# A third staging buffer, and one buffer for the transposed maxima and the value rows

## The chip, the cores and the metric

The kernel runs on one core of a Trainium2 chip. The metric is the device time of one execution in microseconds (us). Three timed executions of the kernel before gave 720.60, 721.52 and 723.17 us, so the median is 721.52 us. Times of single instructions and waits come from one further execution that was profiled.

## The reference, cut to what matters

One decoder block on 1024 tokens and 16 meta tokens, with a model width of 1024. Everything is float32.

```python
h = rmsnorm(concat(meta, x), norm_g)                 # 1040 x 1024
proj = h @ w_in                                      # 1040 x 5128
u, z, q, k, v, z_attn, f, g_pool, g_attn = split(proj)
y_pool = causal_multiscale_pool(u, pool_w, pool_scale) * silu(z)
logit[t, s] = q_t.k_s / 8 + sum_{s<j<=t} log_sigmoid(f_j + b)    # 8 heads of 64, causal
y_attn = softmax(logit) @ v * silu(z_attn)
merged = sigmoid(g_pool) * (y_pool @ w_up_pool) + sigmoid(g_attn) * (y_attn @ w_up_attn)
out = rmsnorm(h_residual + merged @ w_out, final_norm_g)          # the 1024 token rows
```

## The kernel before, in words

A float32 product is computed as three reduced-precision products of a high and a low part of each operand, so every operand is split into `hi` and `lo`. A projection of a 128-column chunk of `w_in` (`g_proj`, L170) is 24 matmuls into one PSUM bank. PE's program order is written out by the kernel itself. The other engines' order comes from a scheduler, and each engine works through its own order without overtaking.

**Attention phase** (about 80 to 425 us). The 16 units are (head pair, head of the pair, half of the 1024 queries). For a unit, `qk` (L710, L711) makes the scores of one key block, ACT and DVE bring them into `S`, and DVE keeps a running maximum in a PSUM tile `pt` (L724). Then `maxes` reduces it over the keys:

- DVE transposes the maxima into the SBUF tile `mt` (L729), reduces them (L734), and with small copies by ACT (`mx` L736, `my` L739) and DVE (`mz` L740) makes the column maxima, which DVE transposes back into a PSUM tile (L742).
- `soft` subtracts that (L751), takes the exponential on ACT (L752) and splits the result into `ph` (L756) and `pl` (L757). `av` (L775) multiplies by the values into the PSUM tile `po`.
- `finish` copies `po` into the SBUF tile `t` on ACT (L786; for the last head pair L783 and L784), and SP stores `t` to DRAM in one or two DMAs of 128 KB (L788, `sp_y<-t`). Those are the value rows.

`maxes` of the next unit stands ahead of `finish` of the present one. So in the order of the program each `mt` is followed by a `t`, and the `t` of a unit is stored to DRAM during the whole following unit. `mt` and `t` have one 2 KB buffer each (per partition) in the pool `ap`.

**The filler.** Between the attention matmuls PE works off a list of projections (class `Fill`): for a later head pair `q` (L268, L272), `k` (L286 on ACT, L290 on DVE) and `v`, and, when none of these is due, the pieces of `u` (`f_u`, L357, L359) and of the gates (`f_raw`, L347, L348). A `u` or gate piece is evicted by ACT into a staging tile `st` and stored from there by SP. There are two staging buffers, in the pool `stg`. The filler's PSUM banks are the two of the pool `pj`, so a bank is used again by the second projection after it, once the evictions (for `k` those of L286 and L290) are through.

**After the attention** the pools `ap` and `at` are closed and the pool `bp` takes their place in SBUF. The gate products (L1049) follow. Their first 48 matmuls use weights that were split during the attention phase. The next ones use weights that ACT splits into `gw` (L1004), with the low part from GpSimd (L1011) or DVE (L1008). DVE also transposes and sums the softmax denominators, which SP brings back from DRAM (`zp<-accd`, L955, L960, L961).

DMAs that add in DRAM are issued by GpSimd (L616, L643), each after the transposition `mt` of a unit; ACT issues copies DRAM to DRAM (L612).

The lines that the change touches:

```python
    spill, stores, evacs = {}, [], []                                     # L338
            st = stg.tile([128, 512], F32, name="st")                     # L346, in f_raw
            st = stg.tile([128, 512], F32, name="st")[:, :c1 - c0]        # L356, in f_u
            mt = ap_.tile([KB, 512], F32, name="mt")                      # L728, in maxes
            t = ap_.tile([128, 512], F32, name="t")                       # in finish, as it was
```

Of the kernel before, what the change touches and what calls it, by code (L numbers as in the profile page):

```python
# [8 lines left out]
F32 = mybir.dt.float32  # L9
# [13 lines left out]
KB = 128  # L23
# [30 lines left out]
def tile_hybrid_block(ctx, tc, x, meta, norm_g, w_in, b_forget, pool_w, pool_scale,  # L54
# [21 lines left out]
    stg = ctx.enter_context(tc.tile_pool(name="stg", bufs=2))  # L76
# [3 lines left out]
    ap_ = A.enter_context(tc.tile_pool(name="ap", bufs=1))  # L80
# [81 lines left out]
    def w_chunk(col, **kw):  # L162
        return split_w([w_in2[:, :, col:col + 128]], **kw)
# [20 lines left out]
    def g_proj(w, t0, t1):  # L184
        wh, wl = w
        ps = fill_bank()[:, :t1 - t0]
        yield from g_mm3(ps, [(wh[:, k, :], wl[:, k, :], hh[k][:, t0:t1], hl[k][:, t0:t1]) for k in range(KO)])
        return ps
# [69 lines left out]
    def keys_of(t0, t1):  # L258
        r = [(0, min(t1, SEQ) - t0, t0 + NM)]
        if t1 > SEQ:  # L260
            r.append((SEQ - t0, t1 - t0, 0))
        return [(slice(a, b), slice(d, d + b - a)) for a, b, d in r]
# [72 lines left out]
            if c0:  # L335
                yield from v_blocks(p, *{384: (1, 2), 768: (3, 4, 5)}[c0])

    spill, stores, evacs = {}, [], []  # L338

    def f_raw(key, col):  # L340
        w = w_chunk(col)
        dt = dr.tile([128, SEQ], F32, name=f"sp_{key[0]}{key[1]}")
        spill[key] = dt
        for c0, c1 in HALVES:
            ps = yield from g_proj(w, c0, c1)
            st = stg.tile([128, 512], F32, name="st")  # L346
            evacs.append(nc.scalar.activation(st, ps, AF.Copy))  # L347
            stores.append(nc.sync.dma_start(dt[:, c0:c1], st))  # L348

    def f_u(g):  # L350
        w = w_chunk(COL_U + g * 128)
        dt = dr.tile([128, L], F32, name=f"sp_u{g}")
        spill["u", g] = dt
        for c0, c1 in PIECES:
            ps = yield from g_proj(w, c0, c1)
            st = stg.tile([128, 512], F32, name="st")[:, :c1 - c0]  # L356
            nc.scalar.activation(st, ps, AF.Copy)  # L357
            for c, d in keys_of(c0, c1):
                last = nc.sync.dma_start(dt[:, d], st[:, c])  # L359
            stores.append(last)  # L360
# [314 lines left out]
    class Unit:  # L675
# [49 lines left out]

        def maxes(self, extra=0.0, hook=None):
            F.pull(LM1 + extra)
            mt = ap_.tile([KB, 512], F32, name="mt")  # L728
            tr = nc.vector.transpose(mt, self.m)  # L729
            if hook is not None:  # L730
                hook(tr)
            r, r2 = self.m[:, :16], self.m[:, 16:32]
            x, y, mx = [sm.tile([128, 16], F32, name=n) for n in ("mx", "my", "mz")]
            nc.vector.tensor_reduce(r, mt.rearrange("p (j b) -> p j b", b=32), axis=AX.X, op=ALU.max)  # L734
            for a, b in ((0, 64), (64, 0)):
                nc.scalar.activation(x[a:a + 64], r[b:b + 64], AF.Copy)  # L736
            nc.vector.tensor_tensor(r2, r, x, op=ALU.max)
            for a, b in ((0, 32), (32, 0), (64, 96), (96, 64)):
                nc.scalar.activation(y[a:a + 32], r2[b:b + 32], AF.Copy)  # L739
            nc.vector.tensor_tensor(mx, r2, y, op=ALU.max)  # L740
            self.pm = psT.tile([128, 512], F32, name="pt")
            nc.vector.transpose(self.pm, mx[:, :, None].to_broadcast([128, 16, 32]))  # L742
            F.pull(LM2)
# [62 lines left out]
    for g in (3, 2, 1, 0):  # L806
        F.add_free(f_u(g))
    for key in raws:
        F.add_free(f_raw(key, cols[key[0]] + 128 * key[1]))
# [679 lines left out]
```

## Time and profile before

| what | value |
|---|---|
| median of three timed executions | 721.52 us (720.60 to 723.17) |
| the profiled execution's own time | 722.44 us |
| its span, first to last instruction | 720.4 us |
| PE busy / weight loads busy | 707.4 us (98%) / 610.7 us (85%) |
| DVE / ACT / GpSimd busy | 512.0 / 425.9 / 353.9 us |
| chain that ended last, share of PE | 94% |

The span leaves 2.0 us of the execution's own time outside, before the first and after the last instruction. Rows of the timeline give start, duration, engine, line, operation, output and input tile, and in brackets how long the engine had been idle and what released it. Rows of the waits give who waited for whom, the total, how often, and the longest.

### The profile page before, as it was taken

How to read it: one execution, taken by the hardware profiler on the slowest of the kernel's cores; microseconds unless marked ns; L12 is line 12 of the kernel's file. 1: busy time of each engine (PE TensorE's matmuls, PEld its weight loads, DVE VectorE, ACT ScalarE, POOL GpSimd, SP SyncE). 2: the span in 40 equal slices, each digit the busy share in tenths (PEclk: the TensorE clock that was granted, in tenths of full speed). 3: DMA queues.
4: the chain of work that ended last, by engine and by line, in shares of the span. 5: the costliest groups of instructions: out<-in, count | busy, mean ns of one | idle time of the engine just before them, and what ended most of it. 6: DMA issues, size and time to landing. Idle time of an engine off the chain costs nothing.

```text
span 720.4 us, 10921 instructions
## 1 busy us (share of the span) xinstructions
PE 707.4 (98%) x3613; PEld 610.7 (85%) x3613; DVE 512.0 (71%) x909; ACT 425.9 (59%) x936; POOL 353.9 (49%) x481
## 2 busy tenths in 40 slices
PE   8999999799999999999999999999999999999996
PEld 6997999798889988898888888888888888888885
DVE  5743488477688767787587866899847545888775
ACT  7753577567787867777587614455646332535445
POOL 5412336477377675747388643458951010007152
PEclk9999999999999999999999999999999999999999
DMA  9211225986968889497858768799518366861006
GB/s 308 65 30 30 60 62 199 271 244 193 260 177 230 239 229 281 118 261 214 224 154 206 223 202 318 239 304 308 129 35 273 113 224 233 272 224 60 0 1 233
DMA packets 97482, 134.09 MB, mean 186 GB/s; under 512 B 11809, under 2 KB 63009, under 8 KB 95154
## 3 DMA queue, kind: packets, MB, share of 16 engines
q1 hardware_dynamic: 83296, 94.07, 40.8%
q0 software_dynamic: 2512, 18.35, 13.3%
q10 hardware_dynamic: 11618, 20.98, 8.2%
q8 instruction: 28, 0.46, 0.2%
q14 instruction: 28, 0.23, 0.1%
HBM read 103.29 MB, written 62.59 MB: 230 GB/s over the span
## 4 chain that ended last, share of the span: by engine, by line
PE 94%; ACT 2%; DMA 2%; DVE 1%; issue 1%; POOL 0%; POOLq 0%; ACTq 0%
PE pj L170 55%; PE pj L1049 12%; PE pj L1369 8%; PE po L775 5%; PE pt L1049 4%; PE pt L1369 2%; PE ps L711 2%; DMA sp_u<-st 2%; PE ps L710 2%; PE pj L521 1%; PE pt L232 1%; PE pj L711 1%; PE pj L710 1%; ACT qa L268 1%; PE pn L232 0%
## 5 line engine op out<-in xcount | busy, mean ns | idle before, releaser
L170 PE MATMUL pj<-hh,whi 128*128 128x512 f32 (+3 forms) x576 | 128.3, 350 | 0.0
L170 PE MATMUL pj<-hh,wlo 128*128 128x512 f32 (+3 forms) x576 | 127.1, 346 | 0.0
L170 PE MATMUL pj<-hl,whi 128*128 128x512 f32 (+3 forms) x576 | 126.8, 345 | 0.0
L170 PEld LDWEIGHTS pj<-hh,whi 128*128 128x128 f32 x576 | 98.4, 190 | 10.2 <-ACT hh L234 0.4
L158 POOL TENSOR_TENSOR wlo<-raw,whi 128x256 fp32r<-128x256 f32 x100 | 73.5, 774 | 65.1 <-PE pj L170 24.5
L170 PEld LDWEIGHTS pj<-hh,wlo 128*128 128x128 f32 x576 | 96.8, 188 | 10.0
L765 POOL TENSOR_TENSOR acc<-acc,S 128x256 f32<-128x256 f32 (+2 forms) x128 | 90.3, 723 | 30.5 <-ACT S L752 20.8
L170 PEld LDWEIGHTS pj<-hl,whi 128*128 128x128 f32 x576 | 96.6, 189 | 9.8
L757 DVE TENSOR_TENSOR pl<-S,ph 128x512 fp32r<-128x512 f32 (+4 forms) x112 | 80.5, 736 | 19.4 <-ACT ph L756 18.9
L1011 POOL TENSOR_TENSOR gw<-graw,gw 128x256 fp32r<-128x256 f32 x52 | 53.6, 1056 | 44.2 <-ACT gw L1004 41.8
L1049 PE MATMUL pj<-gh,gw 128*128 128x512 f32 x276 | 64.3, 389 | 0.0
L724 DVE TENSOR_TENSOR pt<-pt,S 128x400 f32<-128x400 f32 (+2 forms) x96 | 46.4, 483 | 22.1 <-ACT S L715 19.6
L1049 PEld LDWEIGHTS pj<-gh,gw 128*128 128x128 f32 x276 | 51.8, 188 | 10.9
L752 ACT ACTIVATE S<-S 128x512 f32<-128x512 f32 (+4 forms) x112 | 50.6, 479 | 8.6 <-DVE S L751 8.4
L756 ACT ACTIVATE ph<-S 128x512 fp32r<-128x512 f32 (+4 forms) x112 | 52.4, 482 | 2.3 <-PE po L775 1.4
L751 DVE TENSOR_TENSOR S<-S,pt 128x512 f32<-128x512 f32 (+4 forms) x112 | 49.7, 498 | 0.6
L1262 DVE TENSOR_TENSOR rl<-pj,rl 128x512 f32<-128x512 f32 x32 | 22.0, 689 | 28.7 <-PE pj L170 28.1
L1004 ACT ACTIVATE gw<-graw 128x512 fp32r<-128x512 f32 x38 | 23.5, 626 | 27.9 <-DMA graw<-gs 12.0
L715 ACT ACTIVATE S<-ps,negc 128x16 f32<-128x16 f32 (+4 forms) x65 | 33.0, 513 | 10.9 <-PE ps L711 10.3
L765 POOL TENSOR_TENSOR acc<-S 128x256 f32<-128x256 f32 (+1 forms) x32 | 28.6, 926 | 21.1 <-ACT S L752 17.5
L136 POOL TENSOR_TENSOR X<-G 128x256 f32<-128x256 f32 x8 | 5.8, 740 | 63.9 <-DVE G L1264 63.9
L775 PE MATMUL po<-ph,V 128*128 128x512 f32 (+4 forms) x112 | 36.6, 327 | 0.3 <-ACT ph L756 0.2
(250 smaller groups left out, 1434.2 us busy)
## 6 DMA issues: line engine op xcount, KB each, us to landing
raw<-in_w_in_dram SPq DMA_DIRECT2D x27, 512.0 KB, 5.9
gs<-in_w_in_dram ACTq DMA_DIRECT2D x15, 512.0 KB, 7.6
gs<-gs POOLq DMA_DIRECT2D x4, 1536.0 KB, 12.7
graw<-gs SPq DMA_DIRECT2D x12, 512.0 KB, 6.1
td<-in_w_out_dram ACTq DMA_DIRECT2D x10, 512.0 KB, 11.4
graw<-in_w_in_dram SPq DMA_DIRECT2D x9, 512.0 KB, 6.9
xt<-in_x_dram SPq DMA_DIRECT2D x8, 512.0 KB, 6.3
accd<-acc SPq DMA_DIRECT2D x16, 256.0 KB, 4.2
```

What stands on the lines that cost most here:

```text
L158: ins = nc.gpsimd.tensor_tensor(lo[:, k:k + 2], raw[:, k:k + 2], r32(hi[:, k:k + 2]), op=ALU.subtract)
L170: nc.tensor.matmul(ps, a, b, start=(i == 0), stop=(i == len(seq) - 1))
L724: nc.vector.tensor_tensor(m[:kb, c0:], m[:kb, c0:], s[:kb, c0:], op=ALU.max)
L751: nc.vector.tensor_tensor(s[:kb, c0:], s[:kb, c0:], self.pm[:kb, c0:], op=ALU.subtract)
L752: exps.append(nc.scalar.activation(s[:kb, c0:], s[:kb, c0:], AF.Exp))
L756: nc.scalar.activation(ph[:kb, c0:], s[:kb, c0:], AF.Copy)
L757: dves.append(nc.vector.tensor_tensor(pl[:kb, c0:], s[:kb, c0:], r32(ph[:kb, c0:]), op=ALU.subtract))
L765: accs.append(nc.gpsimd.tensor_tensor(acc[:kb, c:c1], (S0 if b == 1 else acc)[:kb, c:c1], s[:kb, c:c1], op=ALU.add))
L775: nc.tensor.matmul(self.po[:, c0:], v, self.P[b][i][:kb, c0:], start=(b == 0 and i == 0), stop=(b == self.nb - 1 and i == 1))
L1011: nc.gpsimd.tensor_tensor(op[:, 1, k:k + 2], raw[:, k:k + 2], r32(op[:, 0, k:k + 2]), op=ALU.subtract)
L1049: nc.tensor.matmul(ps, stat(n, i, p, k), op_h[n][q][k // 2][:, k % 2], start=fresh and m == 0, stop=m == 11, skip_group_check=True)
L1369: nc.tensor.matmul(ps, pick(A_, k, p)[:, i * 128:(i + 1) * 128], pick(B_, k, q)[:, c0:c1], start=start and n == 0, stop=n == 11, skip_grou ...
```

## The change

A counter hands out the staging tiles of `f_u` and `f_raw` in turn: two of three from the pool `stg` as before, every third one from a new 2 KB buffer in the pool `ap`. To make room, the tile `mt` of `maxes` takes the tag of the tile `t` of `finish`, so that both now live in one buffer.

```diff
-    spill, stores, evacs = {}, [], []
+    spill, stores, evacs, staged = {}, [], [], [0]
+
+    def stage_in():
+        staged[0] += 1
+        if staged[0] % 3:
+            return stg.tile([128, 512], F32, name="st")
+        return ap_.tile([128, 512], F32, name="st", bufs=1)
...
-            st = stg.tile([128, 512], F32, name="st")
+            st = stage_in()
...
-            st = stg.tile([128, 512], F32, name="st")[:, :c1 - c0]
+            st = stage_in()[:, :c1 - c0]
...
-            mt = ap_.tile([KB, 512], F32, name="mt")
+            mt = ap_.tile([KB, 512], F32, name="mt", tag="t")
```

Lines behind the change have numbers higher by 6 in the changed kernel. The instructions are the same, and on PE, DVE, ACT and GpSimd they stand in the same order. What differs is what they wait for, and one place on SP. Three places show it. In brackets stand the semaphores that a row waits for; those named DMAHW count landed DMAs of SP and ACT.

The first is DVE's order at the twelfth unit's maxima, where a `k` projection's evictions (`ka`) follow the transposition `mt`. Before:

```order
L724 TENSOR_TENSOR pt_3795<-pt_3795,S_3926 128x16 [waits DVE_49]
L729 STREAM_TRANSPOSE mt_4002<-pt_3795 128x512 [waits DVE_49]
L734 TENSOR_REDUCE pt_3795<-mt_4002 128x16 [waits DVE_49]
L290 TENSOR_TENSOR ka_3778<-pj_3854,ka_3778 64x384 [waits PE_49,Activation_49]
L290 TENSOR_TENSOR ka_3779<-pj_3854,ka_3779 64x384
L737 TENSOR_TENSOR pt_3795<-pt_3795,mx_4005 128x16 [waits DVE_49,Activation_49]
```

The same place in the changed kernel:

```order
L730 TENSOR_TENSOR pt_3795<-pt_3795,S_3926 128x16 [waits DVE_49]
L735 STREAM_TRANSPOSE mt_4002<-pt_3795 128x512 [waits DMAHW3_49,DMAHW2_49,DVE_49]
L740 TENSOR_REDUCE pt_3795<-mt_4002 128x16 [waits DVE_49]
L290 TENSOR_TENSOR ka_3778<-pj_3854,ka_3778 64x384 [waits PE_49,Activation_49]
L290 TENSOR_TENSOR ka_3779<-pj_3854,ka_3779 64x384
L743 TENSOR_TENSOR pt_3795<-pt_3795,mx_4005 128x16 [waits DVE_49,Activation_49]
```

The transposition now waits for two landed DMAs, which are the two stores of the `t` before it (L788), because it writes into the buffer that they read. From the third to the sixteenth unit every `mt` has this wait.

The second is ACT's order at the end of the attention phase: the last three gate pieces and the first two weight splits behind them. Before:

```order
L347 ACTIVATE st_5174<-pj_5111 128x512 [waits DMAHW4_49,PE_49]
L347 ACTIVATE st_5213<-pj_5188 128x512 [waits DMAHW7_49,PE_49,Activation_49]
L347 ACTIVATE st_5241<-pj_5216 128x512 [waits DMAHW4_49,PE_49,Activation_49]
L1004 ACTIVATE gw_5320<-graw_5273 128x512 [waits DMAHW5_49,DMAHW6_49,DMAHW1_49,Pool_49]
L1004 ACTIVATE gw_5341<-graw_5273 128x512 [waits DMAHW3_49,DVE_49]
```

The same place in the changed kernel:

```order
L353 ACTIVATE st_5174<-pj_5111 128x512 [waits DMAHW2_49,PE_49]
L353 ACTIVATE st_5213<-pj_5188 128x512 [waits DMAHW4_49,PE_49]
L353 ACTIVATE st_5241<-pj_5216 128x512 [waits DMAHW7_49,PE_49,Activation_49]
L1010 ACTIVATE gw_5320<-graw_5273 128x512 [waits DMAHW3_49,DMAHW1_49,DMAHW5_49,DVE_49,DMAHW6_49,Activation_49,Pool_49]
L1010 ACTIVATE gw_5341<-graw_5273 128x512
```

The last two gate pieces wait for an earlier store than before (the third store back instead of the second). The first `gw` now also waits for the store of the last gate piece, `st_5241` (DMAHW6 here), because the new staging buffer lies under it.

The third is SP's order at the same time. Before:

```order
L348 DMA sp_ga2_5017<-st_5174 128x512
L955 DMA zp_5264<-accd_771 128x1024
L955 DMA zp_5266<-accd_771 128x1024
L348 DMA sp_ga3_5187<-st_5213 128x512
L348 DMA sp_ga3_5187<-st_5241 128x512
L992 DMA graw_5345<-in_w_in_dram 128x4x256
```

The same place in the changed kernel:

```order
L354 DMA sp_ga2_5017<-st_5174 128x512
L354 DMA sp_ga3_5187<-st_5213 128x512
L354 DMA sp_ga3_5187<-st_5241 128x512
L961 DMA zp_5264<-accd_771 128x1024
L961 DMA zp_5266<-accd_771 128x1024
L998 DMA graw_5345<-in_w_in_dram 128x4x256
```

The first two loads of `zp` moved behind the last two gate stores.

## The prediction

> **What bounds the kernel now.** I read the page first, then the waits, then the timelines of the stretches where the change acts. The chain of waits is PE's almost alone, and PE's own list of waits shows how little it stands still (who waited for whom, us in total, times, longest):
>
> ```profile
> PE 94%; ACT 2%; DMA 2%; DVE 1%; issue 1%; POOL 0%; POOLq 0%; ACTq 0%
> PE pj L710 <- ACT S L715: 4.1, 1, 4.1
> PE po L775 <- ACT ph L756: 0.2, 1, 0.2
> ```
>
> So an edit pays only if it removes one of PE's few waits, and it costs as soon as it delays something that PE needs by more than that thing's lead. Staging is waited for here (waits of ACT, then from the rows of the staging line who waited for it):
>
> ```profile
> ACT st L347 <- DMA sp_ga<-st: 11.2, 2, 5.7
>   PEld pj L1049: 0.2, 1
> ```
>
> ACT stood 11.2 us, but in two places only, and PE's weight loads lost 0.2 us by it. ACT and PE at that place:
>
> ```profile
> 425.63 0.60 ACT L347 ACTIVATE st<-pj 128x512 f32<-128x512 f32 x1 [5.54 <-DMA sp_ga<-st]
> 431.92 0.60 ACT L347 ACTIVATE st<-pj 128x512 f32<-128x512 f32 x1 [5.70 <-DMA sp_ga<-st]
> 428.12 1.98 PE L170 MATMUL pj<-hh,wlo 128*128 128x512 f32 x8
> 441.05 1.09 PE L1049 MATMUL pj<-hh,gw 128*128 128x512 f32 x4
> ```
>
> The last projection ends at 430.1 (428.12 + 1.98); the first product on a fresh `gw` starts at 441.05, and in between PE works on weights that were split earlier. ACT splits `gw` right behind its row at 431.92, so `gw` has a lead of over 7 us.
>
> **What the third buffer removes.** The gate piece at 425.63 would wait for PE alone, the last one for PE at 430.1 instead of a landing at 431.9. Nothing that PE needs is late today except that 0.2 us. Gain: 0.2 us, at most.
>
> **What the shared buffer adds.** `mt` must wait until the stores of the previous `t` have landed, and behind `mt` in DVE's queue stands everything else of DVE. The lead is read by setting each pair of stores against the next `mt`. For all pairs together, then for the pairs before 313.8, 273.0 and 233.4, the rows of the store's line give first and last issue, and time to landing (min/median/max):
>
> ```profile
> DMA to landing us min/median/max: 2.4/9.4/17.4
> ...
> L788 SPq DMA_DIRECT2D sp_y<-t x2: 451/564/676, 299.7 to 300.2; - x2
> DMA to landing us min/median/max: 16.3/16.8/17.4
> ...
> L788 SPq DMA_DIRECT2D sp_y<-t x2: 452/918/1384, 258.7 to 259.2; - x2
> DMA to landing us min/median/max: 14.7/14.7/14.7
> ...
> L788 SPq DMA_DIRECT2D sp_y<-t x2: 544/566/587, 219.2 to 219.8; - x2
> DMA to landing us min/median/max: 13.7/13.8/13.8
> ```
>
> DVE at these places, and, at the last of them, ACT's links of the chain and PE's users:
>
> ```profile
> 233.37 0.72 DVE L729 STREAM_TRANSPOSE mt<-pt 128x512 f32<-128x512 f32 x1
> 273.03 0.72 DVE L729 STREAM_TRANSPOSE mt<-pt 128x512 f32<-128x512 f32 x1
> 313.78 0.72 DVE L729 STREAM_TRANSPOSE mt<-pt 128x512 f32<-128x512 f32 x1
> 315.26 1.13 DVE L290 TENSOR_TENSOR ka<-pj,ka 64x384 fp32r<-64x384 f32 x2
> 316.63 0.73 ACT L739 ACTIVATE my<-pt 32x16 f32<-32x16 f32 x4 [1.00 <-DVE pt L737]
> 319.06 0.91 ACT L286 ACTIVATE ka<-pj 64x256 fp32r<-64x256 f32 x4
> 320.00 1.03 DVE L290 TENSOR_TENSOR ka<-pj,ka 64x256 fp32r<-64x256 f32 x4 [0.35 <-ACT ka L286]
> 317.63 1.57 PE L170 MATMUL pj<-hh,whi 128*128 128x384 f32 x8
> 321.81 1.55 PE L170 MATMUL pj<-hh,whi 128*128 128x384 f32 x8
> 321.06 1.14 ACT L756 ACTIVATE ph<-S 128x512 fp32r<-128x512 f32 x2
> 325.06 0.39 PE L775 MATMUL po<-ph,V 128*128 128x512 f32 x1
> ```
>
> *At 313.8.* The later store lands at 300.2 + 17.4 = 317.6, so `mt` starts 3.8 us late. Queued behind it are the two `ka` evictions, which end at 316.4 (315.26 + 1.13) today and at 320.2 then. They free the PSUM bank that PE's next projection wants at 317.63: PE stands 2.6 us. The `ka` at 320.00 follows on `mt` through a chain without slack: DVE's maxima, ACT's `my` at 316.63, which waits for them, ACT's next rows up to its part of `ka` at 319.06, and DVE's wait for that. So it ends at 321.0 + 3.8 = 324.8, and it frees the bank for 321.81: PE's total delay becomes 324.8 − 321.8 = 3.0 us. The first attention product has its `ph` by 322.2 and takes it at 325.06; that lead of 2.9 covers the 0.8 us that DVE and ACT are then later than PE.
>
> *At 273.0.* The later store lands at 259.2 + 14.7 = 273.9: `mt` is 0.9 us late. The way to PE, in rows of ACT and PE:
>
> ```profile
> 277.58 0.63 ACT L752 ACTIVATE S<-S 128x512 f32<-128x512 f32 x1 [0.45 <-DVE S L751]
> 279.63 1.20 ACT L268 ACTIVATE qa<-pj 64x512 fp32r<-64x512 f32 x2 [0.23 <-PE pj L170]
> 290.21 0.63 ACT L756 ACTIVATE ph<-S 128x512 fp32r<-128x512 f32 x1
> 290.90 0.49 PE L775 MATMUL po<-ph,V 128*128 128x512 f32 x1
> ```
>
> ACT's exponential at 277.58 waits for DVE and takes over the 0.9; the idle 0.23 at 279.63 swallows some. From there ACT and DVE follow each other almost without a gap up to `ph`, which ends at 290.84 just before PE takes it at 290.90 (the 0.2 us in PE's list). So about 0.6 us reach PE.
>
> *At 233.4.* Landing at 219.8 + 13.8 = 233.6, 0.2 us late, less than the 0.8 us of lead at the worst place above: nothing. The other stores landed before their `mt`.
>
> The value of 3.8 is the one that this execution shows; it isn't a constant. From below, if the stores at 299.7 took the 14.7 us of the next slowest pair, `mt` would be 1.1 us late and PE 0.3. From above, I allow each landing 1 us more, about a fourteenth of it: the two terms become 4.0 and 1.6 us, 5.6 together.
>
> **What else moves.** The first two `zp` loads go out behind the last gate store, at about 431, and that store must land before the first `gw`. Rows of DVE, of PE, and of the DMA issues between 404 and 480 (KB each, median us to landing):
>
> ```profile
> 433.01 1.25 DVE L960 STREAM_TRANSPOSE zp<-zp 128x1024 f32<-128x1024 f32 x1 [7.77 <-DMA zp<-accd]
> 452.35 0.69 DVE L1060 TENSOR_TENSOR za<-pj,za 128x512 f32<-128x512 f32 x1
> 456.50 1.98 PE L1049 MATMUL pj<-hh,gw 128*128 128x512 f32 x8
> zp<-accd SPq DMA_DIRECT2D x8, 512.0 KB, 5.9
> sp_ga<-st SPq DMA_DIRECT2D x7, 256.0 KB, 4.9
> ```
>
> `zp` lands at about 431 + 5.9 = 437 and DVE's first transposition starts 4 us later than at 433.01. The eviction that PE needs first behind it is that at 452.35, for the bank that it takes within the row at 456.50: 453.0 + 4 is just early enough, and the waits for later `zp` loads in between shrink the 4. The gate store, issued at about 430.9, lands at about 436, so `gw` is ready by 437.5, against 441.05. Both cost nothing, with 3 us of cover for `gw`: were the landing 9.5 us or more, PE would pay what exceeds that.
>
> **The sum**, made on the profiled execution (722.44, 0.9 above the median): −0.2 + 0.6 + 3.0 = +3.4, so 725.8 there, and 721.5 + 3.4 = 724.9 by the median. PE has no later wait that could give it back. About 0.3%, 2.2 us, is what a measurement of this kernel can tell from no change.
>
> **Rivals.**
>
> *The stores land in time.* In the timed executions the two stores before the twelfth `mt` land by 314.5 (in 14.3 us), where the lead of 0.8 us covers the rest. This place decides: below about 16.5 us to landing the loss is under 2.2 us, below 14.3 it is nothing. Time: 721.3 to 723.7, at the same 721.5 if all is covered. For it: the median of all pairs is 9.4 us, and the 17.4 is the largest of all. Against it: 14.7 and 13.8 occur as well, and the order of all DMAs up to there is unchanged. The Trainium skill ("SBUF — State Buffer", The DMA setup-cost knee) puts a transfer at about 2 us plus its bytes over 436 GB/s; by that estimate a 128 KB store lands within 2.3 us, no `mt` ever waits, and the sum is −0.2. The trace's 2.4 to 17.4 us disagree except at their lowest.
>
> *PE's pause drops its clock.* The one long pause of PE is followed by a slower clock (busy times of PE, weight loads, DVE, ACT, GpSimd, then the granted clock, DMA share and GB/s):
>
> ```profile
> 135.00:140.00 5.00, 1.42 (x8) 0.97 (x6) 0.00 (x0) 0.20 (x1) 0.00 (x0) 1.00 0.98 325
> 140.00:145.00 5.00, 4.46 (x15) 4.16 (x16) 2.10 (x3) 4.28 (x9) 1.34 (x3) 0.66 1.07 321
> ```
>
> The wait of 4.1 us cost 5 x (1 − 0.66) = 1.7 us more. A pause of 2.6 us is shorter, and nothing here shows whether it is enough; with it the sum is +5.1, 726.6. The Trainium skill ("TensorE: Matmul & The Clock Gate", Part 1) gives an idle window of about 3.4 us on a free-running grid as the condition; by that rule the 2.6 us would pass unpunished, and a landing 1 us later might not. The 4.1 us agree with it.
>
> *The freed ACT pays.* If PE's pace at 425 to 440 hung on ACT after all, up to 5.5 us could come back, 716 to 719. Against it stand the 0.2 us and PE's unbroken rows there.
>
> **How the numbers follow.** The forecast, a loss of 2.2 to 5.6 us with the clock kept: 0.56, time 724.9. Landing in time: 0.33. Clock dropped or a late gate store: 0.08, 726 to 728.5. The freed ACT: 0.03. The range goes from 721.3 (all covered, 0.2 gained) to 728.5 (the upper bound of both terms, 5.6, and a part of the clock's 1.7). Faster 0.03, same 0.33, slower 0.64. The likeliest case alone spans 723.7 to 727.1.
>
> **What would show it.** In the profile after: a wait of DVE at `mt` for `sp_y<-t` near 313.8 of 3 to 4 us and near 273 of about 1; in PE's waits a new row for DVE's `ka` (L290) of about 2.6 us; PE's later rows all later by about 3.4 us; ACT's waits for `sp_ga<-st` gone or below 2 us, with a wait at `gw` for the last gate store in their place. I am wrong if `mt` shows no wait, or if PE's rows from 430 on are not later than before; if PE waits between 430 and 470, the third part failed.

## The result, and the profile after

The change makes the kernel slower, by more than was forecast: 728.79 us (727.92 to 729.83, four executions) against 721.98 us, a ratio of 1.0088 with a 95% interval of 1.0074 to 1.0101. On another chip it was 730.93 against 723.62 us, 1.0101 (1.0079 to 1.0123). The ratios are estimated from the single executions and are not the quotient of the two medians (here 1.0094); "us slower" below goes by the ratio. Two executions, one each of two experiments, took over 1000 us at a mean granted clock of 0.56 and 0.61, and the ratios leave them out. The forecast was 724.9, with a range up to 728.5.

The profiled execution after took 728.66 us, with a span of 726.7 against 720.4. PE's own list of waits (who waited for whom, us in total, times, longest):

```profile
PE pj L716 <- ACT S L721: 3.3, 1, 3.3
PE po L781 <- ACT ph L762: 2.3, 2, 2.1
PE pj L1055 <- DVE gx L1066: 1.4, 1, 1.4
PE pn L425 <- DVE car L563: 1.3, 1, 1.3
PE pj L170 <- DVE ka L290: 1.2, 2, 1.0
```

The first and the fourth row were there before (4.1 and 1.3). New are a long wait for `ph` (0.2 before), one for `ka`, and one for `gx`, which no step of the prediction had. The timeline of DVE shows where the first two come from, and that of PE where they arrive:

```profile
274.68 0.72 DVE L735 STREAM_TRANSPOSE mt<-pt 128x512 f32<-128x512 f32 x1 [2.37 <-DMA sp_y<-t]
...
318.91 0.72 DVE L735 STREAM_TRANSPOSE mt<-pt 128x512 f32<-128x512 f32 x1 [2.29 <-DMA sp_y<-t]
320.38 1.12 DVE L290 TENSOR_TENSOR ka<-pj,ka 64x384 fp32r<-64x384 f32 x2
```

```profile
292.19 0.50 PE L781 MATMUL po<-ph,V 128*128 128x512 f32 x1 [2.11 <-ACT ph L762]
...
321.65 1.65 PE L170 MATMUL pj<-hh,whi 128*128 128x384 f32 x8 [0.99 <-DVE ka L290]
```

Both transpositions wait for the value stores, at the two units that were named. At the tenth PE pauses 2.1 us where 0.6 was expected, at the twelfth 1.0 where 2.6 was. What followed the first pause is seen in stretches of 2 us (busy times of PE, weight loads, DVE, ACT, GpSimd, then granted clock, DMA share, GB/s):

```profile
290.00:292.00 2.00, 0.08 (x1) 0.00 (x0) 1.60 (x3) 1.98 (x5) 0.51 (x1) 1.00 0.08 27
292.00:294.00 2.00, 1.81 (x8) 1.57 (x9) 2.00 (x6) 2.00 (x8) 1.92 (x3) 0.85 0.00 0
294.00:296.00 2.00, 2.00 (x8) 1.80 (x8) 2.00 (x4) 1.50 (x5) 1.89 (x4) 0.50 0.00 0
296.00:298.00 2.00, 2.00 (x8) 1.67 (x8) 1.93 (x7) 0.00 (x0) 1.87 (x4) 0.80 0.15 56
```

The clock fell to a half for 3.4 us: 2 x (0.15 + 0.50 + 0.20) = 1.7 us lost on top of the pause.

The third new wait lies where the prediction had stopped looking. SP's timeline at the end of the attention phase, first of before, then of after:

```profile
425.81 1.32 SPq L955 DMA_DIRECT2D zp<-accd  x2
...
469.31 0.36 SPq L966 DMA_DIRECT2D sums<-ge  x1
...
476.80 1.94 SPq L970 DMA_DIRECT2D fin<-sums  x4
```

```profile
435.74 0.93 SPq L961 DMA_DIRECT2D zp<-accd  x2
...
475.51 0.48 SPq L972 DMA_DIRECT2D sums<-ge  x1
...
483.42 1.93 SPq L976 DMA_DIRECT2D fin<-sums  x4
```

And DVE, of before and of after, with PE's row of after behind them:

```profile
481.53 0.61 DVE L974 TENSOR_REDUCE fin<-fin 128x64 f32<-128x256 f32 x1 [0.94 <-DMA fin<-sums]
...
483.50 1.28 DVE L1060 TENSOR_TENSOR gx<-pj,gx 128x512 f32<-128x512 f32 x2
```

```profile
440.56 1.25 DVE L966 STREAM_TRANSPOSE zp<-zp 128x1024 f32<-128x1024 f32 x1 [10.75 <-DMA zp<-accd]
...
487.99 0.62 DVE L980 TENSOR_REDUCE fin<-fin 128x64 f32<-128x256 f32 x1 [2.10 <-DMA fin<-sums]
...
489.96 1.28 DVE L1066 TENSOR_TENSOR gx<-pj,gx 128x512 f32<-128x512 f32 x2
```

```profile
490.79 8.44 PE L1055 MATMUL pj<-gh,gw 128*128 128x512 f32 x36 [1.44 <-DVE gx L1066]
```

The first two `zp` loads leave SP 9.9 us later than before, of which 4.6 is the delay that PE has there already. The first transposition of `zp` starts at 440.6 instead of 433.0. The later loads win back part of it, but the sums still go out 6.2 us late and come back 6.5 us late at `fin` (487.99 against 481.53), 1.6 and 1.9 more than PE's own 4.6. In DVE's queue stands `gx` behind `fin`, and PE needs its bank: 1.4 us.

ACT is freed at 425 to 437 as forecast. The last gate piece waits for PE alone, and `gw` waits for that piece's store:

```profile
434.74 0.60 ACT L353 ACTIVATE st<-pj 128x512 f32<-128x512 f32 x1 [4.89 <-PE pj L170]
437.92 1.16 ACT L1010 ACTIVATE gw<-graw 128x512 fp32r<-128x512 f32 x2 [2.58 <-DMA sp_ga<-st]
```

No wait of PE answers to either. In sum: 1.9 + 1.7 at the tenth unit (the 0.2 that PE waited there before taken off), 1.2 at the twelfth, 1.4 at `gx`, less 0.8 at 136 to 140, where a store of `u` happened to land earlier. That makes 5.4 of the 6.3 us. With PE's instructions of the two profiles set against each other one by one, the rest lies mostly at the same places: the twelfth unit adds 1.7 us in all (its second `ka` makes the row at 321.81 of before start at 326.30) and `gx` 1.7.

### The profile page after: what moved, and what is told of

It is laid out like the page before. It is cut to its first block, busy times and chain, and to the rows that moved or that the text cites. A ratio compares the mean times of both kernels' runs of the same rounds, so it can differ in the third digit from the quotient of the medians.

```text
span 726.7 us, 10931 instructions
## 1 busy us (share of the span) xinstructions
PE 710.0 (98%) x3613; PEld 613.1 (84%) x3613; DVE 511.3 (70%) x909; ACT 425.3 (59%) x936; POOL 353.5 (49%) x481
## 4 chain that ended last, share of the span: by engine, by line
PE 87%; DMA 5%; DVE 2%; ACT 2%; issue 1%; SPq 1%; POOL 0%; POOLq 0%; ACTq 0%; DVEq 0%
PE pj L170 52%; PE pj L1055 9%; PE pj L1375 8%; PE po L781 5%; PE pt L1055 3%; DMA sp_y<-t 2%; PE pt L1375 2%; PE ps L717 2%; DMA sp_u<-st 1%; PE ps L716 1%; DMA sums<-ge 1%; PE pj L527 1%; PE pt L232 1%; PE pj L717 1%; PE pj L716 1%
## 6 DMA issues: line engine op xcount, KB each, us to landing
td<-in_w_out_dram ACTq DMA_DIRECT2D x10, 512.0 KB, 11.2
```

## The experiments

Each was timed beside the kernel before on its chip (723.0 to 723.6 us there).

**The change once more.**

> The changed kernel once more, beside the others on one chip. Expected: 5 to 7 us slower than before, as when it was first measured; in its profile the pauses of PE near 290 and 321 again add up to 3 to 5 us, split otherwise than 2.1 and 1.2, and the wait for gx near 490 is between 0 and 3.4 us.

Measured: 1.0101 (1.0079 to 1.0123), 7.3 us slower, a little above what was expected. Its PE list has 2.4 (2.2 the longest) for `ph`, 2.4 for `ka` and 2.5 for `gx`, and of these three pauses only the one for `ka` was followed by a slower clock. The places are the same in both profiles; how much each costs is not.

**The two halves of the change.** One kernel shares the buffer only, the other adds the third buffer only.

```
shared only:   mt = ap_.tile([KB, 512], F32, name="mt", tag="t")     # st as before
third only:    mt = ap_.tile([KB, 512], F32, name="mt", tag="pl", bufs=NPH + 1)
               # st handed out in turn as in the change
```

> Only the shared buffer of mt and t; two staging buffers as before. Theory A (the shared buffer costs most of it): the tenth and the twelfth mt wait for the value stores by 0.9 to 2.5 us and 2.3 to 3.8 us, PE loses about 3.6 us at the first place (1.9 of pause, 1.7 of slower clock, if its pause is as long as in the changed kernel) or 0.6 (if it is as short as forecast) and 1.8 to 3.0 at the second: 3.4 to 5.4 us slower than before, 725.4 to 727.4. Rival B (the third buffer and the new order on SP make things late): at most 1.5 us slower, under 723.5.

Measured: 728.25 us, 1.0070 (1.0058 to 1.0083), 5.1 us slower, with these rows of PE:

```profile
PE pj L710 <- ACT S L715: 4.5, 1, 4.5
PE pj L170 <- DVE ka L290: 3.2, 1, 3.2
PE po L775 <- ACT ph L756: 1.6, 2, 1.5
```

This time the pause at the twelfth unit is the long one, 3.2 us, close to the forecast's 3.0, and the clock fell behind it, not behind the 1.5 us at the tenth.

> Only the third staging buffer: mt takes a place in the ring of pl, whose readers are matmuls, so that mt waits for no store. Theory A: no wait of DVE at mt for a store; what is left is the pair of zp loads behind the gate stores, which comes out at the softmax sums as a wait of PE of 1.4 us near 485: 0.7 to 1.7 us slower than before, 722.7 to 723.7. Rival B: 4 us slower or more, 726 and above.

Measured: 725.16 us, 1.0026 (1.0009 to 1.0043), 1.9 us slower, spread from 721.9 to 730.4 over 12 executions. The profiled one is the slowest of them. Rows of DVE and PE:

```profile
438.55 1.25 DVE L966 STREAM_TRANSPOSE zp<-zp 128x1024 f32<-128x1024 f32 x1 [11.44 <-DMA zp<-accd]
...
487.33 0.58 DVE L980 TENSOR_REDUCE fin<-fin 128x64 f32<-128x256 f32 x1 [3.68 <-DMA fin<-sums]
```

```profile
490.10 10.07 PE L1055 MATMUL pj<-gh,gw 128*128 128x512 f32 x32 [3.44 <-DVE gx L1066]
```

No `mt` waits for a store. Of the 8.2 us that this profile is longer than that of before, 6.3 arise at `gx`: a pause of 3.4 us, and the clock at a half for 6.8 us behind it. Another 1.8 arise behind the pause at 136, which before has too; there the clock stayed low for 6.8 us instead of 3.4. The halves add up: 5.1 + 1.9 = 7.0, between the two measurements of the change (6.4 and 7.3). Rival B, that the third buffer costs most of it, falls.

**The order on SP.** The very last gate piece takes a buffer of the old ring, once in the change, once with the third buffer alone; SP's order is then that of before.

```diff
-        if staged[0] % 3:
+        if staged[0] % 3 or staged[0] == 36:
```

> The change, but the very last gate piece takes a buffer of the old ring, so that SP issues the first two zp loads ahead of the last two gate stores, as before. Theory A: the wait of PE for gx near 490 is gone, the two places of mt stay: 1.4 to 1.7 us faster than the changed kernel, 4.5 to 5.0 slower than before. Rival: the wait for gx is only the tail of the delay made by mt, and stays: as slow as the changed kernel, 6.3 to 6.8 slower than before.

Measured: 1.0077 (1.0064 to 1.0090), 5.6 us slower, and no wait of PE for `gx` in its list. Against the 7.3 of the change measured again (on another chip) that is 1.7 less, as expected; the total is above the 4.5 to 5.0, which was reckoned from one profile. The pauses at the two places of `mt` are 2.7 and 1.4 us here.

> Only the third staging buffer, with mt in the ring of pl, and the very last gate piece in the old ring, so that SP's order is that of before. If the order of SP at the end of the attention phase is all that the third buffer costs: the same as before, within 0.3%, and no wait of PE for gx. Rival (the buffer, or mt in the ring of pl, costs something else): 1 to 2 us slower, as with the third buffer alone.

Measured: 0.9998 (0.9989 to 1.0007). No wait for `gx` is in PE's list. So the third buffer's cost is the order of two loads and two stores on SP, and `mt` in the ring of `pl` costs nothing.

**Each place by itself.** The shared buffer for one unit's `mt`, or for all but one.

```diff
-            mt = ap_.tile([KB, 512], F32, name="mt")
+            mt = ap_.tile([KB, 512], F32, name="mt", tag="t" if <this unit> else "mt")
```

> Before, with one difference: the tenth mt alone sits in the buffer of t, so that of all mt only this one waits for the value stores. Theory A (each place costs by itself, by the landing of its own stores): DVE waits 0.9 to 2.4 us there, PE pauses 0.6 to 2.1 us near 290 and no other place changes; 0.6 to 1.6 us slower where the clock keeps, up to 3.6 where it drops. Rival (the places act on each other: PE is made early or late by the other waits): 0.3 us or less, all of it covered.

> Before, with the twelfth mt alone in the buffer of t. Theory A: DVE waits 3.5 to 4.5 us there (more than in the changed kernel, since nothing has made DVE late before), PE pauses 2.5 to 3.2 us near 320 and its clock drops after that: 3 to 5 us slower than before. Rival (the stores of t land late only when the earlier places have shifted them into the next transfers): a wait under 1.5 us and at most 1 us slower.

> Only the shared buffer, with two staging buffers, but the twelfth mt keeps a buffer of its own. If the places add up: the shared buffer at all units cost 5.1 us and at the twelfth alone 4.1, so 0 to 1.5 us slower than before, 723.4 to 725; the tenth mt waits 0.3 to 2.4 us and PE pauses up to 2.2 us near 290, without a slower clock in most executions. Rival (the twelfth wait took over what the tenth would cost, by the slower clock that only one of them can bring on): 2 to 3.6 us slower.

> Only the shared buffer, with two staging buffers, but the eighth mt keeps a buffer of its own. Theory C (the wait of 0.4 us at the eighth mt, which costs PE nothing by itself, makes the next unit's sums and value stores later, and these are what the tenth mt then waits for): the tenth mt waits under 1 us, PE has no pause near 290, and the time is that of the twelfth place alone, 3.5 to 3.8 us slower than before. Rival (the tenth wait is the landing of its own stores and nothing else): it waits 1.6 us or more and PE pauses 1.4 us near 290, 4.8 us slower, as with the shared buffer everywhere.

| `mt` that waits | ratio (95%) | us slower |
|---|---|---|
| tenth alone | 1.0001 (0.9990 to 1.0012) | 0.1 |
| twelfth alone | 1.0057 (1.0043 to 1.0070) | 4.1 |
| all but the twelfth | 1.0025 (1.0014 to 1.0035) | 1.8 |
| all but the eighth | 1.0051 (1.0034 to 1.0069) | 3.7 |
| all (shared only, above) | 1.0070 (1.0058 to 1.0083) | 5.1 |

The twelfth place carries the loss. Its PE row, and the clock behind it in stretches of 3.5 us:

```profile
321.84 2.01 PE L170 MATMUL pj<-hh,whi 128*128 128x384 f32 x8 [3.12 <-DVE ka L290]
```

```profile
318.00:321.50 3.50, 0.72 (x6) 0.49 (x5) 2.33 (x4) 0.36 (x2) 0.82 (x1) 1.00 0.70 210
321.50:325.00 3.50, 3.16 (x13) 3.19 (x14) 2.56 (x6) 2.95 (x10) 1.59 (x3) 0.70 1.08 185
325.00:328.50 3.50, 3.50 (x18) 3.50 (x17) 3.15 (x8) 3.45 (x9) 3.20 (x5) 0.81 0.95 248
```

A pause of 3.1 us, and 3.5 x (0.30 + 0.19) = 1.7 us by the clock: 4.8 in the profile, 4.1 by the ratio. The tenth place alone costs nothing (its `mt` waited 0.3 us), so that the places do not simply add up. With the other units waiting as well (all but the twelfth) the tenth `mt` waited 3.0 us, PE paused 2.5 and the clock fell; that profile is the slowest of 11 executions, and the 1.8 us of the table lie between the two expectations. I took the eighth for the reason: a wait that costs PE nothing would still make the next unit's stores later. The run without the eighth speaks against that as the whole reason, since its tenth `mt` still waited 1.5 us and PE paused 1.3. Its time, though, is nearer to the twelfth's alone, and the intervals overlap.

The traces show two parts of it. With PE's own delay taken off, the ninth `mt`, which sets off a large add in DRAM (see below), comes 0.9 to 1.4 us later than in before wherever the eighth waits, and 0.1 later in the run without the eighth. And that add takes 16.1 us to landing with the tenth alone and 16.5 to 17.5 where all or all but one wait (14.8 to 17.6 in all profiles that have it). Both move the tenth's wait, which was 0.3 to 3.0 us; what spreads the landing stays open.

**Why the stores land late.** The change without two of GpSimd's adds in DRAM.

```diff
-        7: [(add, GS[1], GS[5]), (n12, 2), ...
+        7: [(n12, 2), ...
-        9: [(add, GS[3], GS[5]), (put, TD[2], WB["11"])],
+        9: [(put, TD[2], WB["11"])],
```

> The change without two of GpSimd's DMAs that add in DRAM (1.5 MB each, issued near 256 and 298), so two of the sums of weight blocks are left out of the computation. Theory A with its cause (these transfers hold up the value stores issued just behind them): the stores of those two units land within 10 us instead of 15 to 17, neither mt waits for them, and the time is 1 to 2 us above before, 723 to 724. Rival (the stores are late because of their place on SP's queue or of all the other traffic): they still take 14 us or more, mt still waits 2 us at both places, and the time is 4.5 us or more above before.

Measured: 1.0016 (1.0003 to 1.0029), 1.2 us slower, and the waits of `mt` are down to one of 0.5 us, at the eighth. The rows of the store's line for the tenth and then the twelfth `mt`, in the change and in this kernel (first and last issue, then time to landing, min/median/max):

```profile
L794 SPq DMA_DIRECT2D sp_y<-t x2: 853/1138/1422, 258.9 to 259.8; - x2
...
DMA to landing us min/median/max: 14.8/14.8/14.8
...
L794 SPq DMA_DIRECT2D sp_y<-t x2: 452/520/589, 301.6 to 302.1; - x2
...
DMA to landing us min/median/max: 15.9/16.3/16.6
```

```profile
L794 SPq DMA_DIRECT2D sp_y<-t x2: 451/524/596, 260.4 to 260.9; - x2
...
DMA to landing us min/median/max: 2.5/2.5/2.5
...
L794 SPq DMA_DIRECT2D sp_y<-t x2: 451/559/667, 300.2 to 300.7; - x2
...
DMA to landing us min/median/max: 7.8/8.6/9.4
```

And GpSimd's add ahead of the tenth in the change:

```profile
L622 POOL DMA_DIRECT2D gs<-gs x1: 834/834/834, 256.5 to 256.5; - x1
...
DMA to landing us min/median/max: 17.4/17.4/17.4
```

That add lands at 256.5 + 17.4 = 273.9 and the store at 259.8 + 14.8 = 274.6. The store is small and late because it was issued behind 1.5 MB: without that add it lands in 2.5 us. (Leaving the add out takes its traffic away too; whether its place or its bytes hold the store up, this run doesn't tell apart.) At the twelfth a second add of 0.5 MB (`sp_y<-sp_y`) stays ahead of the stores, and they still take 7.8 to 9.4 us. And each of the two large adds is issued 2.8 us behind an `mt`: the transposition sets off the transfer that holds up the stores that the next `mt` waits for. The Trainium skill ("SBUF — State Buffer", The DMA setup-cost knee) gives about 2 us plus the bytes over 436 GB/s, by which 2.3 us is the estimate for 128 KB. The 2.5 us at the tenth agree with it, the other landings here do not.

**A version that gains.** In before, PE's longest pause comes from ACT, which stands 7.6 us at the issue of a copy, behind a late store of `u`:

```profile
139.19 0.50 ACTq L612 DMA_DIRECT2D td<-in_w_out_dram  x1
139.79 0.69 ACT L715 ACTIVATE S<-pj,negc 128x512 f32<-128x512 f32 x1 [7.55 <-DMA sp_u<-st]
```

The copy waits for the semaphore that it counts up itself when it lands. The store of `u` that SP issued at 128.03 counts the same one, though the two share no data. Here GpSimd issues two of those copies, first with two staging buffers, then with three.

```diff
-        (put, TD[5], WB["12"])
+        (put, TD[5], WB["12"], "pool")
-                after(nc.scalar.dma_start(*puts.pop(0)), exps[-1])
+                d, s, by = puts.pop(0)
+                after((nc.gpsimd if by == "pool" else nc.scalar).dma_start(d, s), exps[-1])
```

> Before, with two of the copies DRAM to DRAM of the third unit issued by GpSimd in place of ACT. In before ACT stands 7.6 us at such an issue, behind a late store of u, and PE pauses 4.1 us at 136 to 140 and then runs at a lower clock. If that issue is the whole cause: the pause is gone, and 4 to 6 us are gained, 717.5 to 719.5 where before is 723.5. If the late store also holds the staging buffer that ACT needs next: a pause of 1 to 3 us stays and 1 to 3 us are gained.

Measured: 1.0013 (1.0003 to 1.0023), so nothing was gained, less than either expectation. The pause at 136 is gone and another stands 16 us behind it. A row of PE's list, and ACT's rows:

```profile
PE pj L170 <- ACT st L357: 4.8, 2, 4.5
...
140.03 0.49 ACT L357 ACTIVATE st<-pj 128x384 f32<-128x384 f32 x1 [2.24 <-DMA sp_u<-st]
...
156.39 0.40 ACT L357 ACTIVATE st<-pj 128x272 f32<-128x272 f32 x1 [6.01 <-DMA sp_u<-st]
```

PE lost 4.5 us there, waiting for an eviction that waits for a staging buffer. This is a place at which a third buffer is needed:

> The kernel of the run above, and the two copies of the third unit issued by GpSimd. With two staging buffers those copies took the pause at 136 away and ACT's wait for a staging buffer gave it back at 151 to 157 (PE 4.5 us). If a third buffer is what was lacking there: both pauses gone, 4 to 6 us faster than before, 718 to 719.5. Rival (stores of u land so late that the third buffer is waited for too, or another wait takes over): at most 1.5 us faster.

Measured: 718.18 us against 723.36, a ratio of 0.9920 (0.9902 to 0.9938), with `mt` in the ring of `pl` and the last gate piece in the old ring. PE's first rows:

```profile
PE po L783 <- ACT ph L764: 1.4, 3, 0.8
PE pn L426 <- DVE car L564: 1.3, 1, 1.3
```

Both pauses are gone, and PE's clock stays up from 125 to 155. With these copies moved, the third buffer takes the ratio from 1.0013 to 0.9920; without them it had nothing to give.

## Why the prediction was wrong

- *What the third buffer removes* (0.2 us at most): right. ACT's 11.2 us of waits went and PE did not notice. The rival of the freed ACT is dead.
- *At 313.8* (3.0 us): the path was right, the price too low. The pause alone measured 3.1 us, and the slower clock behind it, a rival with a share of 0.08, came with it: 4.1 us for this place alone. In the profile of the change shown first the pause was only 1.0 us: DVE came there 2.8 us later than before (316.6 against 313.8), the stores had gone out 1.9 us later (302.1 against 300.2), and they landed in 16.6 us instead of 17.4.
- *At 273.0* (0.6 us): nothing alone, up to 2.5 us of pause with the clock on top when other units wait too. I took the issue and landing of the stores, and DVE's arrival, from before as they stood. In the profile shown first the stores landed 0.7 us later (274.6 against 273.9) and DVE came 0.7 us earlier (272.3 against 273.0), since PE had stood 0.8 us less at 136: 2.4 us of wait instead of 0.9. The path from there to PE was right.
- *At 233.4* (nothing): DVE waited 0.4 to 0.9 us there; PE lost nothing at that place, but the wait moved the ninth `mt` and the add behind it, which the forecast left out.
- *What else moves* ("Both cost nothing"): the failed step. I followed the two `zp` loads as far as the first evictions behind them, up to 457, and took it that the delay shrinks away. It shrinks to about 2 us and then passes through `sums`, SP, `fin` and DVE's queue to `gx`, where PE waits at 489, behind the stretch from 430 to 470 that I had named as the place to look: 1.9 us by the ratio. The half about `gw` was right.
- *PE's pause drops its clock* (0.08): mis-sized. Pauses of 2.5 to 3.2 us brought it every time. I had judged by length against the one example of 4.1, and took that to agree with a whole idle window; on the grid of the last section it filled none (1.2 us lay in one stretch, 2.9 in the next).
- *The stores land in time* (0.33): never at the twelfth in any profile in which its `mt` shares the buffer, unless the large add was left out.

By the halves: the shared buffer 5.1 where the forecast had 3.6, the third buffer 1.9 where it had −0.2. Of the 3.6 us that the forecast of 3.4 lacks by this sum, the step on the loads is 2.1 and the size of the shared buffer 1.5.

## What to carry to other kernels

A buffer that is stored to DRAM is not free when its last engine is done, and sharing it turns the landing of a store into a wait of whoever comes next; look up what large transfer is issued just ahead of that store. When loads change places on a queue, follow them to the last one that uses their result, not to the first that hides the delay. A further staging buffer pays only where an eviction waits for staging and PE waits for that eviction: find that row first.

## What the runs showed of the hardware

The clock fell after pauses of PE much shorter than the one in before. All pauses over 0.7 us in the middle of these profiles, with what the clock did behind them:

| pause of PE, us | clock behind it |
|---|---|
| 0.79, 0.99, 1.26, 1.39, 1.44, 1.46 | kept |
| 2.11, 2.35, 2.48 | half for 3.4 us |
| 2.18, 2.45 | kept |
| 2.51, 2.65, 3.12, 3.19 | half for 3.4 us |
| 3.30 to 4.66 (14 pauses) | half for 3.4 us (8) or 6.8 us (6) |

Length alone does not decide between 2.1 and 2.5 us. In each profile the times between changes of the clock are whole multiples of 3.413 us; in the changed kernel the falls at 139.8 and 293.4 us are 45 of them apart. So the changes lie on a grid, and a pause can be set against it. The two nearest cases are the 2.45 (the change once more, clock kept) and the 2.48 (all but the twelfth, clock at a half). For each, the stretch of the grid that holds most of the pause, and the next:

```profile
490.18:493.59 3.41, 1.62 (x8) 1.01 (x6) 2.04 (x5) 1.44 (x2) 1.34 (x2) 1.00 0.94 246
493.59:497.01 3.42, 2.76 (x12) 2.35 (x13) 3.42 (x4) 1.64 (x3) 1.53 (x2) 1.00 1.08 394
```

```profile
292.02:295.43 3.41, 1.59 (x8) 1.38 (x9) 3.36 (x8) 3.41 (x10) 2.21 (x3) 1.00 0.02 8
295.43:298.84 3.41, 3.41 (x12) 2.92 (x11) 3.38 (x10) 1.71 (x7) 3.17 (x7) 0.50 0.00 0
```

PE stood still for 1.79 us of the first stretch and for 1.82 of the second. In all 14 profiles, from the first rise of the clock on, the clock fell behind every stretch with 1.82 us or more of this and behind none with 1.79 or less. Once low, it rose behind the stretches with up to 0.57 us and stayed low behind those with 0.61 or more. The ends of matmuls are modelled in these profiles, so the bounds are theirs and not exact. By them the pause of 2.11, which lay in one stretch, cost a slower clock, and the 2.18, split into 0.54 and 1.64, did not.

The Trainium skill ("TensorE: Matmul & The Clock Gate", Part 1) has a free-running window of 3413 ns behind this, and the grid agrees with it. That the clock falls after an idle window of about 3.4 us does not agree as a condition: a little more than half a window was enough.
